# Six pairs with seven products in every block, other far pairs, and new assumptions of the planner

## The chip, the cores and the metric

The kernel runs on one core of one Trainium2 chip. The metric is the device time of one execution in microseconds (us); where several runs are shown, their median. TensorE (PE) multiplies, VectorE (DVE) and ScalarE (ACT) work on whole tiles, GpSimd (POOL) does small sums and issues some of the transfers, SyncE (SP) issues the others.

## The reference, cut to what matters

Two layers of an encoder trunk on 256 tokens of width 4096. Each layer normalises its input, multiplies it by one wide matrix, runs attention and a two-way retention on the parts of the result, and multiplies what comes out by a second matrix:

```python
for l in range(DEPTH):                       # DEPTH = 2
    h = rmsnorm(x, norm_w[l])
    proj = h @ w_in[l]                       # (256 x 4096) @ (4096 x 11264)
    aq, ak, av, ag, rq, rk, rv, rg = jnp.split(proj, SPLIT_POINTS, axis=-1)
    ...                                      # rotary embedding, 16 query and 4 key heads
    a_out = jax.nn.silu(ag) * gqa_attention(aq, ak, av)
    r = bidirectional_retention(rq, rk, rv, log_gf, log_gb)   # 8 heads
    r_out = jax.nn.silu(rg) * rmsnorm(r, ret_norm[l])
    x = x + jnp.concatenate([a_out, r_out], axis=-1) @ w_out[l]   # (256 x 4096) @ (4096 x 4096)
return rmsnorm(x, final_norm)
```

Everything is float32. The two projections are nearly all of the work, and all 4096 x 15360 weights of a layer are read once.

## The kernel before, in words

**Blocks.** A block of the program makes 256 rows by 1024 columns of a projection. Each layer has 11 blocks for `w_in` and 4 for `w_out`, 30 blocks in all. Within a block the program goes over the 4096 inner rows in 16 pairs of 256 (`NP`, numbered 0 to 15). One pair in one block is a product of two-by-two halves: 2 halves of tokens, 2 of inner rows, 2 of columns.

**Three matmuls for one product.** A float32 factor is split into a high part that TensorE multiplies exactly enough and a low part that is what remains: `whi` and `wlo` of the weights, `x8h` and `x8l` (or `x7h` and `x7l`) of the other operand. A product is high by high, low by high and high by low: two matmuls in line 1458 with `whi`, one in line 1468 with `wlo`, each with 512 columns. Products on the same page are taken up to four together (`TOGETHER`): first the matmuls with `whi` of all four, then those with `wlo`.

**Seven or eight products.** The two-by-two product of a pair takes eight products (`EIGHT_PRODUCTS`) in the plain way, or seven (`SEVEN_PRODUCTS`) with sums of the halves on either side, in the manner of Strassen. The results gather over all pairs in seven accumulators `M1` to `M7`. At the end of a block `combine` adds them up into the pages `ca` and `cb` on DVE. The pairs with seven products need sums of their weights in each block: `Weights.begin` makes `wsum` with one subtraction of 1024 columns and two operations of 512, and their weights then fill four pages (A, T, B with one half, U) in place of two (A, B). Which pairs take seven is written in two names: `SEVEN` holds for all blocks, `MORE` for the blocks of `w_out` alone. `GROUPS` cuts the row of pairs ahead of each pair with seven products, and `pages_of` lays the pages of the other pairs of a group between the four pages of its first.

**Where the parts are made.** A weight page arrives in `wraw` (transfers of SP), ACT copies it to `whi`, DVE subtracts to get `wlo` (`Weights.parts`). Five pages (`RING`) are in hand at a time; when the last product on a page is done, the page five places on is begun. For one page per far pair (`FAR_PAIRS`, page B) DVE does nothing: ACT writes `fhi`, then minus `fhi` into `flo`, and a transfer of POOL's queue adds the weights from memory onto `flo` (`far_parts`, line 505). There is one buffer for such a page (`FAR`).

**The planner.** The program is written out as one fixed order for each engine. While it is written, a clock (`now.t`) and the times until which DVE and ACT are thought busy (`ve.until`, `ac.until`) are kept with assumed costs. After each product `tick` asks `Weights.room` whether a step of other work fits: the splitting of operands, the attention and retention tasks, the postponed `thirds`. `V_FIXED` and `S_FIXED` are the fixed costs of one instruction of DVE and ACT in this reckoning, `STEP_V` and `STEP_S` the time that a step is allowed, `LANDING`, `STORE`, `FETCH` and `FAR_LANDING` the times allowed for transfers, `EARLY` how far ahead of its operands a step may be placed, `ADD_AHEAD` how far ahead of ACT an accumulating transfer may be placed, `TIGHT_A` and `TIGHT_B` the number of products at the start and the end of a block in which steps are held back. The cost of DVE is

```python
return V_FIXED + n * (0.00052 if one else 0.00104)    # one: a copy or an operation with a scalar
```

**Start and end.** In the first block two pairs (`NATIVE`) are multiplied whole, as they come, and the first two blocks (`PLAIN`) do without the split difference `x3` of the operand, which is made later, in steps of `third`. In the last block five pairs (`DELAYED`) keep the weights of their last product in places of operands that are done with; `dead_room` says which.

**Between the layers.** `out_tasks` adds the residual with an accumulating transfer to both pages of a block of `w_out`, and `out_task` then squares, stores and transposes each.

Of the kernel before, what the change touches and what calls it, by code (L numbers as in the profile page):

```python
# [32 lines left out]
NP = KT // 2  # L33
# [6 lines left out]
FAR = 1  # L40

STEP_V = 1.6
STEP_S = 1.3

V_FIXED = 0.15
S_FIXED = 0.12

MM = {512: 0.2268, 256: 0.1177}
PASS = 0.2

LANDING = 11.0
STORE = 8.0
FETCH = 13.0
FAR_LANDING = 11.0
MARGIN = 0.0

RUSH = 1.5

EARLY = 0.7

ADD_AHEAD = 2.5

NEED = {"ak": 4, "ag": 3, "rk": 4, "rg": 4}

PE_REST = 1.5

TIGHT_A = 3
TIGHT_B = 5

AT_ONCE = 2  # L70

# [3 lines left out]

START = 1

SEVEN = (0, 3, 6, 9, 12)

MORE = (1,)  # L80

DELAYED = tuple([_p for _p in range(NP) if _p not in SEVEN + MORE][-5:])

# [5 lines left out]

DEFER = (0,)  # L90

FAR_PAIRS = (2, 5, 8, 11, 14)


AQ, AK, AV, AG, RQ, RK, RVO, RG = 0, 2048, 2560, 3072, 5120, 6144, 7168, 9216
# [75 lines left out]

SEVENS = (SEVEN, tuple(sorted(SEVEN + MORE)))
EIGHTS = [_p for _p in range(NP) if _p not in SEVENS[1]]
# [19 lines left out]
def is_far(group, p, k):  # L193

    return k == PAGE_B and p in FAR_PAIRS

# [14 lines left out]
PLAIN_ORDER = ("M3", "M8", "M4", "M2")  # L211

EASY = ("M7",)

TOGETHER = 4
BANKS = ("M1", "M2", "M3", "M4", "M5", "M6", "M7", "M8")
# [35 lines left out]
def vector_cost(name, n, kwargs):  # L252
    one = name in ("tensor_copy", "tensor_scalar", "tensor_scalar_mul", "tensor_scalar_add", "memset")
    return V_FIXED + n * (0.00052 if one else 0.00104)

# [6 lines left out]
def hybrid_encoder(  # L262
# [15 lines left out]
    now = Now()  # L278
# [16 lines left out]
    def t(pool, shape, tag, bufs=None, dt=F32):  # L295
        kw = {} if bufs is None else {"bufs": bufs}
        return pool.tile(shape, dt, tag=tag, name=tag, **kw)

    def f32(v):
        return v.bitcast(F32)  # L300
# [4 lines left out]
    def own(n):  # L305

        if current[0]:
            current[0].own += n

    def drop(n=1):  # L310

        held[0] -= n
        own(-n)

    def page(shape, name, dt=F32):

        held[0] += 1
        own(1)
        assert held[0] <= PAGES, name
        return sp.tile(shape, dt, tag="pg", name=name, bufs=PAGES)  # L320
# [78 lines left out]
    class Weights:  # L399
# [92 lines left out]
        def far_parts(self, g, src):  # L492
# [6 lines left out]
            for h in halves:  # L499
                ac.activation(g.lo[h], f32(g.hi[h]), AF.Copy, scale=-1.0)  # L500
            g.high_at, g.low_at = ac.until, ac.until + FAR_LANDING

# [50 lines left out]
        def add(self, now_all=False):  # L553

            while self.adds and (now_all or self.adds[0][0] <= now.t + ADD_AHEAD):
                self.adds.pop(0)[1]()

        def room(self, using):
# [13 lines left out]
            if tight[0] and max(ve.until, ac.until) > now.t + 0.3:  # L572
                return False
            return (
                max(ve.until, now.t) + STEP_V + low <= limit
                and max(ac.until + STEP_S, free) + 1.05 + low <= end
            )

    rooms = []

    def dead_room():

        if not rooms:
            e, o = len(EIGHTS), len(SEVENS[1])
            kinds = {
                "x3": ("x3", e, [P, 2, 2, P], "p k s t -> p (k s t)"),
                "x8h": ("x8h", e, [P, 2, SEQ], "p k s -> p (k s)"),
                "x8l": ("x8l", e, [P, 2, SEQ], "p k s -> p (k s)"),
                "x7h": ("x7h", o, [P, 7, P], "p k t -> p (k t)"),
                "x7l": ("x7l", o, [P, 7, P], "p k t -> p (k t)"),  # L590
            }
            order = "x7h x7l x3 x3 x7h x7l x7h x7l x3 x8h x8l x7h x7l x3 x8h x8l x7h x7l x3 x7h" if MORE else "x3 x3 x8h x8l x3 x3 x8h x8l x7l x7h x3 x3 x8h x8l x3 x3 x8h x8l x7l x7h"
            rooms.extend(kinds[v] for v in order.split())
        tag, bufs, shape, flat = rooms.pop(0)
        return t(ap, shape, tag, bufs, F32R).rearrange(flat)[:, :NB]

# [228 lines left out]
    class Lane:  # L825
# [5 lines left out]
        def step(self):  # L831
# [17 lines left out]
            else:  # L849
                self.ready = max(self.last - EARLY, now.t + (rest or 0.1))  # L850

# [64 lines left out]
    def turned(src, room):  # L916

        ve.transpose(
            room.rearrange("p (b k t) -> p b k t", b=4, t=BLK),
            src.rearrange("p m (i b e) -> p b (m i) e", i=4, e=BLK),
        )

    def store(room, to):

        to = to.rearrange("(b e) (a f) -> a e b f", e=BLK, a=4)
        for a in range(4):  # L930
            nc.gpsimd.dma_start(to[a], room[BLK * a : BLK * (a + 1), :].rearrange("e (b f) -> e b f", b=4))
        drop()
# [65 lines left out]
    def rotary(v, L, kind, to):  # L998

        scaled(v, L)  # L1000
        yield
        C, S = L.tables.get(kind) or rope_tables(kind, L.plain)
        v4 = v.rearrange("p m (h d) -> p m h d", h=4)
        if kind in ("aq", "ak"):
            rs = t(sp, [P, 8], "rs", 3)
            for m in range(MT):
                for h in range(4):
                    ac.activation(
                        junk[:, :HD], v4[:, m, h], AF.Square, accum_out=rs[:, 4 * m + h : 4 * m + h + 1]
                    )  # L1010
                yield
            rsqrt(rs, rs, 8, HD)
        o = page([P, MT, NB], "rot")
        o4 = o.rearrange("p m (h d) -> p m h d", h=4)
        for m in range(MT):
            src = v[:, m, :].rearrange("p (h a b e) -> p h a b e", h=4, a=2, b=2)
            dsts = o[:, m, :].rearrange("p (h a b e) -> p h a b e", h=4, a=2, b=2)
            s5 = S[:, m, :].rearrange("p (a b e) -> p a b e", a=2, b=2)
            for h in range(2):
                ve.tensor_mul(  # L1020
                    dsts[:, :, :, h, :],
                    src[:, :, :, 1 - h, :],
                    s5[:, :, h, :].unsqueeze(1).to_broadcast([P, 4, 2, HD // 4]),
                )
            ve.tensor_mul(
                v4[:, m], v4[:, m], C[:, m, :].unsqueeze(1).to_broadcast([P, 4, HD])
            )
            yield
        ve.tensor_add(o, o, v)
        if kind == "ak":  # L1030
            yield
            o8 = o.rearrange("p m (h d) -> p (m h) d", d=HD)
            ve.tensor_mul(o8, o8, rs.unsqueeze(2).to_broadcast([P, 8, HD]))
        yield
        v = v.rearrange("p m n -> p (m n)")
        turned(o, v)
        drop()
        yield 0.0
        store(v, to)
        return rs if kind == "aq" else None  # L1040
# [16 lines left out]
    def attention_pair(g, h, kv, qT, rs, done):  # L1057
# [40 lines left out]
        store(room, p_dram[2 * (g % 2) + h // 2])  # L1098
        yield STORE

# [25 lines left out]
    def attention_group(L, g, gacc, qacc):  # L1126
# [11 lines left out]
        rs = yield from rotary(qacc, L, "aq", q_dram[g % 2])  # L1138
        yield STORE
        L.rs[g] = rs  # L1140
# [206 lines left out]
    def block(after_pair, phase, then, first_order=False, order=LAST_ORDER, last=None, plain=False, hurried=False):  # L1347
# [16 lines left out]
        if not first_order:  # L1364
            for b in reversed(EASY):
                n = next(i for i, v in enumerate(flat) if v[0] == b and v[1] == 0)
# [72 lines left out]
        while n < len(flat):  # L1439
# [5 lines left out]
            for one in group:  # L1445
                m, name, p, index, k, h = one
                tight[0] = m < TIGHT_A or m >= len(flat) - TIGHT_B
                a = begin_product(*one)
# [64 lines left out]
    def load_gain(n):  # L1513
        g = page([P, 2, NB], "gain")
        nc.sync.dma_start(g[:, 0, :], final_norm[columns(n)].partition_broadcast(P))
        return g
# [4 lines left out]
    def out_task(l, n, res):  # L1521

        last = l == DEPTH - 1
        if last:
            fn = load_gain(n)
            outs[n] = res
            own(-1)
            yield LANDING
            room = fn[:, 1:2, :].to_broadcast([P, MT, NB])
            fn = fn[:, 0, :]  # L1530
        else:
            turn = page([P, KG * SEQ], "room")
            room = turn.rearrange("p (m n) -> p m n", m=MT)
        for m in range(MT):
            ac.activation(room[:, m, :], res[:, m, :], AF.Square, accum_out=sums[:, m, n : n + 1])
        yield
        if last:
            ve.tensor_mul(res, res, fn.unsqueeze(1).to_broadcast([P, MT, NB]))
            drop()
            return  # L1540
        if n == N_OUT - 1:
            rstd_of(layers[l + 1], sums[:, :, :N_OUT], N_OUT)
        nc.gpsimd.dma_start(x2_dram[n].rearrange("p (m n) -> p m n", m=MT), res)
        yield
        turned(res, turn)
        if n < N_OUT - 2:
            drop()
            yield 0.0
            store(turn, next_dram[n])
            put(n, None, 2 * l + 2)  # L1550
        else:
            yield LANDING - 2.0
            to = res.rearrange("p m n -> p (m n)")
            yield from move(turn, to)
            drop()
            put(n, to, 2 * l + 2)

    def out_tasks(l, n, c):
        for i in range(2):
            nc.gpsimd.dma_start(c[i], residual(l, 2 * n + i), accum_op=ALU.add)  # L1560
        yield LANDING
        for i in range(2):
            yield from out_task(l, 2 * n + i, c[i])

    def last_combine(res):

# [147 lines left out]
    for l, L in enumerate(layers):  # L1714
        for bi, (one, _) in enumerate(BLOCKS):
# [9 lines left out]
            c = block(after, 2 * l + 1, 2 * l + 1 + (bi == N_IN - 1), start, plain=2 * l in DEFER and bi < PLAIN)  # L1725
# [7 lines left out]
        for n in range(N_OUT2):  # L1733
# [19 lines left out]
            else:  # L1753
                if final:
                    turning.append(Turn(2 * l + 2))
                c = block(after, 2 * l + 2, 2 * l + 2 + (n == N_OUT2 - 1), hurried=n == 0)
# [50 lines left out]
```

## Time and profile before

| | |
|---|---|
| time, median of 3 runs | 2625.7 us (2624.82 to 2630.23) |
| the profiled execution, its own time | 2625.96 us |
| its span, first to last instruction | 2623.8 us |
| mean granted clock of TensorE | 0.998 |
| busy: PE, DVE, ACT, POOL | 2601.0, 2166.6, 1804.2, 372.9 us |
| instructions | 34532 |
| moved by transfers | 683.94 MB, mean 261 GB/s |

The profile names a group of instructions by line, engine, operation and tiles, written out<-in. Everything that goes through the planner's clocks has line 247, so DVE and ACT work is told apart by its tiles. PE is the matmul itself, PEld the loading of its stationary operand. `x1340` is a count, and behind the bar stand the busy time in us, the mean of one in ns, and the idle time of the engine ahead of the group with what ended it. Matmuls overlap, so the duration of one (389 ns) is longer than the time from one to the next. In the views by stretch, each engine has its busy time and in brackets its instructions, then come the granted clock, the busy share of the transfer engines and what they moved.

### The profile page before, as it was taken

How to read it: one execution, taken by the hardware profiler on the slowest of the kernel's cores; microseconds unless marked ns; L12 is line 12 of the kernel's file. 1: busy time of each engine (PE TensorE's matmuls, PEld its weight loads, DVE VectorE, ACT ScalarE, POOL GpSimd, SP SyncE). 2: the span in 40 equal slices, each digit the busy share in tenths (PEclk: the TensorE clock that was granted, in tenths of full speed). 3: DMA queues.
4: the chain of work that ended last, by engine and by line, in shares of the span. 5: the costliest groups of instructions: out<-in, count | busy, mean ns of one | idle time of the engine just before them, and what ended most of it. 6: DMA issues, size and time to landing. Idle time of an engine off the chain costs nothing.

```text
span 2623.8 us, 34532 instructions
## 1 busy us (share of the span) xinstructions
PE 2601.0 (99%) x11725; PEld 2154.2 (82%) x11725; DVE 2166.6 (83%) x2684; ACT 1804.2 (69%) x2576; POOL 372.9 (14%) x510
## 2 busy tenths in 40 slices
PE   9999999999999999999999999999999999999998
PEld 7788888888888888888878888888888888888886
DVE  7898887798778898877978878888887688987876
ACT  8676676667565788655877666776576557876655
POOL 0012211221111101111111111211210111010000
PEclk9999999999999999999999999999999999999999
DMA  9988888887778777889988888888877787788887
GB/s 305 285 262 285 272 271 284 270 269 243 235 238 249 239 249 237 274 262 281 311 246 259 271 274 283 266 273 288 280 231 217 245 258 239 221 259 264 254 249 228
DMA packets 201121, 683.94 MB, mean 261 GB/s; under 512 B 24176, under 2 KB 30832, under 8 KB 200944
## 3 DMA queue, kind: packets, MB, share of 16 engines
q1 hardware_dynamic: 147760, 521.27, 56.3%
q0 software_dynamic: 53184, 160.46, 26.5%
q8 instruction: 92, 1.51, 0.2%
q14 instruction: 85, 0.70, 0.1%
HBM read 637.60 MB, written 44.04 MB: 260 GB/s over the span
## 4 chain that ended last, share of the span: by engine, by line
PE 92%; issue 1%; DMA 1%; ACT 1%; DVE 1%; POOL 0%; POOLq 0%; DVEq 0%; ACTq 0%
PE M L1458 59%; PE M L1468 30%; PE ps L973 1%; PE ps L974 1%; PE ps L975 1%; DMA q<-q_dram 1%; PE ps L1458 0%; DMA wraw<-in_w_in 0%; DVE wlo L247 0%; ACT ca L247 0%; DVE ca L247 0%; PE ps L1468 0%; DVE cb L247 0%; ACT pr L247 0%; ACT whi L247 0%
## 5 line engine op out<-in xcount | busy, mean ns | idle before, releaser
L247 ACT CAST whi<-wraw 128x1024 fp32r<-128x1024 f32 (+1 forms) x808 | 768.7, 962 | 463.0 <-PE M L1458 310.3
L247 DVE TENSOR_TENSOR wlo<-wraw,whi 128x1024 fp32r<-128x1024 f32 (+1 forms) x808 | 886.9, 1110 | 236.6 <-ACT whi L247 230.9
L1458 PE MATMUL M<-whi,x8h 128*128 128x512 f32 x1340 | 521.9, 389 | 0.0
L1458 PE MATMUL M<-whi,x8l 128*128 128x512 f32 x1340 | 521.5, 389 | 0.0
L1458 PE MATMUL M<-whi,x7h 128*128 128x512 f32 x1265 | 493.9, 390 | 3.7 <-DVE ca L247 2.5
L1458 PE MATMUL M<-whi,x7l 128*128 128x512 f32 x1265 | 492.9, 390 | 0.0
L247 ACT CAST whi<-wsum 128x1024 fp32r<-128x1024 f32 x314 | 329.6, 1050 | 137.1 <-PE M L1458 93.8
L1468 PE MATMUL M<-wlo,x8h 128*128 128x512 f32 x1340 | 420.2, 389 | 0.0
L247 DVE TENSOR_TENSOR wlo<-wsum,whi 128x1024 fp32r<-128x1024 f32 x314 | 382.5, 1218 | 38.7 <-ACT whi L247 36.8
L1468 PE MATMUL M<-wlo,x7h 128*128 128x512 f32 x1265 | 407.8, 389 | 1.1 <-DVE wlo L247 1.1
L1458 PEld LDWEIGHTS M<-whi,x8h 128*128 128x128 f32 x1340 | 251.6, 188 | 51.7 <-issue 0.2
L1458 PEld LDWEIGHTS M<-whi,x8l 128*128 128x128 f32 x1340 | 251.6, 188 | 51.7 <-issue 0.2
L1468 PEld LDWEIGHTS M<-wlo,x8h 128*128 128x128 f32 x1340 | 251.2, 188 | 51.7
L1458 PEld LDWEIGHTS M<-whi,x7h 128*128 128x128 f32 x1265 | 237.8, 188 | 55.7 <-DVE ca L247 2.9
L1468 PEld LDWEIGHTS M<-wlo,x7h 128*128 128x128 f32 x1265 | 237.5, 188 | 50.5 <-DVE wlo L247 1.5
L1458 PEld LDWEIGHTS M<-whi,x7l 128*128 128x128 f32 x1265 | 238.0, 188 | 48.9
L1458 PE MATMUL M<-whi,x 128*128 128x512 f32 x840 | 258.9, 389 | 0.7 <-ACT whi L247 0.7
L505 POOL DMA_DIRECT2D flo<-in_w_in x108 | 97.3, 901 | 1044.4 <-ACT flo L247 1001.4
L247 ACT CAST fhi<-wraw 128x1024 fp32r<-128x1024 f32 (+1 forms) x148 | 154.7, 1045 | 99.8 <-PE M L1458 93.9
L247 DVE TENSOR_TENSOR wsum<-wraw 128x1024 f32<-128x1024 f32 x157 | 191.2, 1218 | 18.7 <-DMA wraw<-in_w_out 11.3
L1458 PEld LDWEIGHTS M<-whi,x 128*128 128x128 f32 x840 | 157.1, 188 | 32.9 <-ACT whi L247 1.1
L1458 PE MATMUL M<-fhi,x8h 128*128 128x512 f32 x440 | 171.3, 389 | 0.0
(301 smaller groups left out, 3282.9 us busy)
## 6 DMA issues: line engine op xcount, KB each, us to landing
wraw<-in_w_in SPq DMA_DIRECT2D x700, 512.0 KB, 5.0
wraw<-in_w_out SPq DMA_DIRECT2D x256, 512.0 KB, 5.2
flo<-in_w_in POOLq DMA_DIRECT2D x108, 512.0 KB, 7.9
flo<-in_w_out POOLq DMA_DIRECT2D x38, 512.0 KB, 8.8
full<-next_dram POOLq DMA_DIRECT2D x18, 512.0 KB, 7.7
p_dram<-room POOLq DMA_DIRECT2D x64, 128.0 KB, 4.6
pT<-p_dram POOLq DMA_DIRECT2D x16, 512.0 KB, 8.1
next_dram<-room POOLq DMA_DIRECT2D x40, 128.0 KB, 5.9
```

Source lines behind the costliest of these rows:

```text
L247: return call(out, *args, **kwargs)
L505: nc.gpsimd.dma_start(g.lo[h], g.src[0][:, h, :], accum_op=ALU.add)
L973: nc.tensor.matmul(out, a[0], b[0], start=start, stop=False)
L974: nc.tensor.matmul(out, a[0], b[1], start=False, stop=False)
L975: nc.tensor.matmul(out, a[1], b[0], start=False, stop=stop)
L1458: nc.tensor.matmul(acc[name], a[i], g.hi[h], start=m == first[name] and not i, stop=False)
L1468: nc.tensor.matmul(acc[name], a, g.lo[h], start=False, stop=m == final[name])
```

## The change

Six pairs instead of five take seven products in the blocks of `w_in`, and the blocks of `w_out` have the same six: `SEVEN` becomes (0, 3, 6, 9, 11, 13), `MORE` is empty (before, `w_out` had 0, 1, 3, 6, 9, 12). The far pairs are 2, 5, 8, 12, 15. `dead_room` works out its list of places from the pairs, and `out_tasks` lets the first page go on without the second (with `APART` at zero, both transfers are still issued at once). Nine assumptions of the planner have other values.

```diff
-STEP_S = 1.3
+STEP_S = 1.7
-V_FIXED = 0.15
+V_FIXED = 0.08
...
-STORE = 8.0
+STORE = 6.0
...
-FAR_LANDING = 11.0
+FAR_LANDING = 10.0
...
-EARLY = 0.7
-ADD_AHEAD = 2.5
+EARLY = 0.4
+ADD_AHEAD = 0.5
...
-TIGHT_A = 3
-TIGHT_B = 5
+TIGHT_A = 4
+TIGHT_B = 4
...
-SEVEN = (0, 3, 6, 9, 12)
-MORE = (1,)
+SEVEN = (0, 3, 6, 9, 11, 13)
+MORE = ()
...
-FAR_PAIRS = (2, 5, 8, 11, 14)
+FAR_PAIRS = (2, 5, 8, 12, 15)
...
+APART = 0.0
...
-            order = "x7h x7l x3 x3 x7h x7l ..." if MORE else "x3 x3 x8h x8l ..."
-            rooms.extend(kinds[v] for v in order.split())
+            for p in range(NP):
+                if p not in EIGHTS:
+                    rooms.extend(kinds[v] for v in ("x7h", "x7l"))
+                else:
+                    rooms.extend(kinds[v] for v in ("x3", "x8h", "x8l")[: 3 if p in EIGHTS[2:] and p not in DELAYED else 1])
...
     def out_tasks(l, n, c):
         for i in range(2):
             nc.gpsimd.dma_start(c[i], residual(l, 2 * n + i), accum_op=ALU.add)
-        yield LANDING
-        for i in range(2):
-            yield from out_task(l, 2 * n + i, c[i])
+            if i < 1:
+                yield APART
+        second = now.t + LANDING
+        yield max(0.0, LANDING - APART)
+        yield from out_task(l, 2 * n, c[0])
+        yield max(0.0, second - now.t)
+        yield from out_task(l, 2 * n + 1, c[1])
```

More of the change, by code (lines that the diff above doesn't have):

```diff
@@ L591, in dead_room @@
             }
-            order = "x7h x7l x3 x3 x7h x7l x7h x7l x3 x8h x8l x7h x7l x3 x8h x8l x7h x7l x3 x7h" if MORE else "x3 x3 x8h x8l x3 x3 x8h x8l x7l x7h x3 x3 x8h x8l x3 x3 x8h x8l x7l x7h"
-            rooms.extend(kinds[v] for v in order.split())
+            for p in range(NP):
[3 more added lines that the diff above has]
+                    rooms.extend(kinds[v] for v in ("x3", "x8h", "x8l")[: 3 if p in EIGHTS[2:] and p not in DELAYED else 1])
         tag, bufs, shape, flat = rooms.pop(0)
```

## The prediction

> **What bounds the kernel now.** I read the page first (busy shares and the chain that ended last), then the list of who waited for whom on TensorE, then busy time by stretch, then the groups of instructions by form. From the page:
>
> ```profile
> span 2623.8 us, 34532 instructions
> PE 2601.0 (99%) x11725; PEld 2154.2 (82%) x11725; DVE 2166.6 (83%) x2684; ACT 1804.2 (69%) x2576; POOL 372.9 (14%) x510
> PE 92%; issue 1%; DMA 1%; ACT 1%; DVE 1%; POOL 0%; POOLq 0%; DVEq 0%; ACTq 0%
> ```
>
> TensorE (PE) is busy for all but 22.8 us of the span, and the chain that ended last is 92% TensorE. So the time is the number of matmuls times their spacing, plus few waits. VectorE (DVE) is the second engine, with 457 us free on average over the span. The waits of TensorE:
>
> ```profile
> engine line waited for: us in total, times, longest us
> PE M L1468 <- DVE wlo L247: 2.8, 2, 1.7
> PE M L1458 <- DVE ca L247: 2.5, 3, 1.0
> ...
> PE M L1458 <- DVE cb L247: 1.2, 1, 1.2
> ...
> PE M L1458 <- ACT whi L247: 0.7, 1, 0.7
> ```
>
> `wlo` and `whi` are the low and high halves of a weight page; `ca` and `cb` are the adds that empty the accumulators at the end of a block. These four come to 7.2 us in the whole execution, over 30 blocks. Where the slack of DVE is thin shows by stretch:
>
> ```profile
> core 0: us, PE busy (x) PEld busy (x) DVE busy (x) ACT busy (x) POOL busy (x), PEclk, DMA share, GB/s
> 15.00:40.00 25.00, 25.00 (x101) 18.68 (x100) 24.55 (x39) 23.37 (x42) 1.03 (x1) 1.00 0.97 360
> 40.00:80.00 40.00, 40.00 (x178) 33.14 (x177) 35.07 (x49) 34.10 (x57) 1.74 (x2) 1.00 0.92 292
> 80.00:120.00 40.00, 37.71 (x159) 30.46 (x158) 33.28 (x49) 26.66 (x46) 3.41 (x5) 0.96 0.82 269
> 120.00:160.00 40.00, 40.00 (x178) 33.14 (x177) 37.87 (x70) 27.92 (x48) 5.66 (x6) 1.00 0.88 247
> 160.00:200.00 40.00, 39.41 (x173) 32.02 (x172) 38.61 (x55) 28.77 (x48) 8.40 (x13) 1.00 0.86 264
> ...
> 960.00:1060.00 100.00, 100.00 (x456) 83.19 (x455) 91.07 (x125) 80.71 (x129) 8.98 (x9) 1.00 0.76 237
> ...
> 1345.00:1378.00 33.00, 30.54 (x134) 24.65 (x133) 22.79 (x32) 31.33 (x56) 3.03 (x4) 1.00 0.80 236
> ...
> 2493.00:2558.00 65.00, 65.00 (x288) 53.87 (x287) 48.59 (x51) 36.49 (x39) 5.22 (x6) 1.00 0.84 248
> ```
>
> In the first 200 us, where operands, weights and the postponed thirds are all made, DVE is busy 169.4 of the 185 us from 15 to 200, and there TensorE loses time (80 to 120, 160 to 200). At 960 to 1060, a change of stage, DVE is busy 91 of 100 us and TensorE loses nothing. In a plain stretch (2493 to 2558) DVE has 16 us of 65 to spare.
>
> **Term 1: fewer matmuls.** Before, five pairs take 7 products in blocks of the input projection and a sixth (pair 1) only in those of the output projection; after, six do in both. So each of the 22 input blocks loses one product, which is three matmuls of 512 columns: 22 x 3 = 66. The built programs agree: 11709 matmuls before, 11643 after, and the 66 missing are all 128x512. Their price is the spacing, not their modelled duration: in the row 2493 to 2558, 65.00 us hold 288 matmuls of this size with no gap, 0.2257 us each. 66 x 0.2257 = 14.9 us, all on the path that ends last, since TensorE is that path.
>
> The Trainium skill ("TensorE: Matmul & The Clock Gate", Part 1, on the 56 ns gap) gives 215.7 ns from start to start for a warm matmul of 512 columns; the row's 225.7 ns is higher, so this trace differs. By the page term 1 would be an estimated 14.2 us.
>
> **Term 2: more work on DVE and ScalarE (ACT).** The rows by form that price it:
>
> ```profile
> L247 DVE TENSOR_TENSOR wlo<-wraw,whi 128x1024 fp32r<-128x1024 f32 x643 | 781.9, 1219 | 226.5 <-ACT whi L247 221.3 <-PE M L1458 2.4 <-PE M L1468 0.9
> L247 ACT CAST whi<-wraw 128x1024 fp32r<-128x1024 f32 x643 | 672.5, 1050 | 408.9 <-PE M L1458 263.4 <-DMA wraw<-in_w_in 52.9 <-DMA wraw<-in_w_out 51.0
> L247 DVE TENSOR_TENSOR wlo<-wsum,whi 128x1024 fp32r<-128x1024 f32 x314 | 382.5, 1218 | 38.7 <-ACT whi L247 36.8 <-PE M L1468 1.5
> L247 ACT CAST whi<-wsum 128x1024 fp32r<-128x1024 f32 x314 | 329.6, 1050 | 137.1 <-PE M L1458 93.8 <-DVE wsum L247 37.0 <-PE M L1468 5.1
> L247 DVE TENSOR_TENSOR wsum<-wraw 128x1024 f32<-128x1024 f32 x157 | 191.2, 1218 | 18.7 <-DMA wraw<-in_w_out 11.3 <-DMA wraw<-in_w_in 7.4
> L247 DVE TENSOR_TENSOR wlo<-wraw,whi 128x512 fp32r<-128x512 f32 x165 | 113.0, 685 | 10.1 <-ACT whi L247 9.6 <-issue 0.2
> L247 DVE TENSOR_TENSOR wsum<-wsum,wraw 128x512 f32<-128x512 f32 x157 | 108.7, 692 | 5.5
> L247 DVE TENSOR_TENSOR wsum<-wraw,wsum 128x512 f32<-128x512 f32 x157 | 107.4, 684 | 0.1
> L247 ACT CAST whi<-wraw 128x512 fp32r<-128x512 f32 x165 | 102.0, 618 | 54.1 <-PE M L1458 46.9 <-DMA wraw<-in_w_out 6.7 <-ACT x L247 0.5
> ```
>
> A pair with 7 products needs three sums (1.22 + 0.69 + 0.68 us) and low halves of three and a half pages; a pair with 8 needs two. By count over the built programs DVE gets 22 of each sum, 44 more `wlo<-wsum`, 21 more half pages and 21 fewer whole `wlo<-wraw`: 22 x 2.594 + 44 x 1.218 + 21 x 0.685 - 21 x 1.219 = 99.4 us, or 4.5 us per input block. ACT gets 44 x 1.050 + 21 x 0.618 - 21 x 1.050 = 37.1 us. DVE then stands at 2266 of some 2609 us (87%), ACT at 1841 (71%). On average both still lie beside TensorE and cost nothing. The local sums say where they might not:
>
> - Steady input blocks. An input block of 122 products is 82.6 us of TensorE. Its weights cost DVE 6 x 6.93 (pairs of 7: three sums and 1.22 + 1.22 + 1.22 + 0.69) + 5 x 1.22 (near pages of the far pairs) + 10 x 1.22 = 59.9 us, which leaves 22.7 us for all else (27.8 before). All other DVE work is 2166.6 less 1684.7 (the six DVE rows above), 482 us over 30 blocks, 16 us each. It fits.
> - Neighbours 9, 10, 11, 12. Pairs 9 and 10 cost DVE 6.93 + 2.44 = 9.4 us against 15 products, 10.2 us; pairs 11 and 12 cost 8.2 against 10.2. The output blocks of before had it worse: pair 0 alone is followed by pair 1, also of 7, and pairs 0 to 2 cost 6.93 + 6.93 + 1.22 = 15.1 us of DVE against 22 products, 14.9 us, without TensorE waiting. That neighbourhood is gone, so the output blocks become easier. I take nothing for either.
> - The start. In the built program DVE has, by these durations and for other forms by 0.15 us plus 1.04 ns per element, 10 us more work in front of the adds that close the first block (one more pair of 7, two of the postponed thirds drawn forward, one more operand of 7) and 16 us more in front of those that close the second. Against this stand 5.4 us of free DVE time between 15 and 80, and 15.6 between 15 and 200. This doesn't fit without loss. The bounds are -3.9 us (the existing waits there, 2.3 us at 80 to 120, and 1.6 us of clock, both vanish) and +10.1 us (all of the first excess is waited for). I take +3: 10 us less the 5.4 free and less about 2 us, one page of lead, since five pages are kept in hand.
>
> The clock belongs to this place. In the row 80 to 120 its mean is 0.96; over 40 us that is 3.2 us at half rate, so 1.6 us lost, behind the 2.3 us of waits in the same row. The row 1345 to 1378 has 2.5 us of waits and a clock of 1.00, so such waits don't always do it, and I add nothing. The Trainium skill ("TensorE: Matmul & The Clock Gate", Part 1, what is happening) says that the clock halves after an idle window of about 3.4 us; this trace shows a halving behind shorter waits, so it doesn't fully agree. By the page, longer waits at the start would make halvings likelier.
>
> **Term 3: what is moved.** The far pairs become 12 and 15 in place of 11 and 14, still five per block, so the transfers stay the same in number. The relevant rows, and the last line of the answer on tile `flo`:
>
> ```profile
> 301.91 0.39 PE L1468 MATMUL M<-flo,x8h 128*128 128x512 f32 x1
> 302.52 1.06 ACT L247 ACTIVATE flo<-fhi 128x1024 fp32r<-128x1024 f32 x1
> 303.88 0.88 POOL L505 DMA_DIRECT2D flo<-in_w_in  x1 [12.55 <-ACT flo L247]
> 316.87 0.62 PE L1468 MATMUL M<-flo,x8h 128*128 128x512 f32 x2
> DMA to landing us min/median/max: 5.2/8.0/10.4
> ```
>
> There is one buffer for a far page. It comes free at 302.3, is refilled by ACT and an accumulating transfer issued at 303.88, and is needed at 316.87. The slowest landing (10.4) ends at 314.3. From 12 to 15 there are the same 19 products, but the last pair takes its products one by one, so the low half is needed six matmuls (1.35 us) earlier: 315.5. It still lands 1.2 us early, hidden by those 19 products; if ACT is late there, the cost is that lateness. ADD_AHEAD of 0.5 moves the issue behind at most 2 us of planned work on POOL's queue, which the median landing covers (311.9). Splitting out_tasks in two lets the first page go on as before and the second wait for its own landing: no matmul stands behind it. Steps for the last block's kept pages and pair 1's operands are exchanged like for like: nothing.
>
> The other constants change only where the planner places steps. V_FIXED of 0.08 makes it believe a 1024-wide subtraction takes 0.08 + 1024 x 0.00104 = 1.145 us, where the row says 1.219. So it packs DVE tighter than it runs, 0.07 us per instruction. Bounds: below, the 7.2 us of waits go; above, rival two. I take 0, because in the built program the DVE work between the first and the last accumulator add of a block falls from 239 to 212 us in sum over the 30 blocks: the page sums that stood between them moved away.
>
> **Sum.** The profiled execution took 2625.96 us, 2.2 more than its span, and 0.3 more than the median of 2625.7. 2625.96 - 14.9 + 3.0 = 2614.1; less 0.3, the median should be 2613.8. A measurement of this kernel can tell about 0.2% (5.2 us) from no change.
>
> **Rivals.** One: DVE is late at the start and also where stages change, and eats most of the gain. For it: the sums of the start, and 1345 to 1378, where 2.5 us were lost already. Its price is 10.1 us at the start, at most 16 with the second block's excess: 2621 to 2627. Against it: 960 to 1060, where 91% on DVE cost nothing. Two, on the other side: the planner's short price of DVE makes the accumulators come free late at every block. For it: `ca` and `cb` waits exist (3.7 us over 30 blocks, 0.12 each), and 93 DVE instructions a block times 0.07 us are 6.5 us unplanned. One add of 0.68 us late at each of 30 boundaries is 20.4 us: 2613.8 - 3 + 20.4 = 2631. It decides from 0.67 us per block on, where term 1 and the 5.2 us are used up. Against it: DVE idles 457 us, mostly behind `whi`, and catches up in those gaps, and fewer sums lie between the adds. That the change doesn't remove the products is ruled out by the built program.
>
> **How the numbers follow.** Forecast (start between -4 and +7): 0.80. Rival one: 0.12, two thirds of it within 0.2%. Rival two: 0.08. The range runs from 2607 (term 1 whole, and half of the 7.2 us of waits and of the clock's loss gone, -4) to 2621 (the first excess wholly waited for). Faster by over 0.2%: 0.80 and a third of rival one, less some for both in part, 0.83; within 0.2%: 0.09; slower: 0.08.
>
> **What would show it.** Right: 66 fewer matmuls, DVE busy near 2266 and ACT near 1841 us, TensorE idle 23 to 29 us with the new idle time before 200 us, `flo` waits near zero, DVE waits at block ends below 0.3 us each. Wrong: `ca`, `cb` or `wlo` waits of over 0.6 us in most blocks, clock below 1.00 after 130 us, or a `flo` wait once per block at pair 15 or pair 2.

## The result and the profile after

The changed kernel is slower: 2641.1 us (median of 4 runs) against 2625.3, a ratio of 1.0056 with a 95% interval of 1.0035 to 1.0077. That is 14.7 us slower by the ratio, where 11.9 us faster was forecast. One of the four runs (2814.4 us, at a mean clock of 0.87) was in a slower state of the chip and is left out of the ratio; the median of the other three is 2640.2 us. The profiled execution took 2642.1 us. From its page:

```profile
span 2640.3 us, 34679 instructions
...
PE 2595.8 (98%) x11659; PEld 2143.2 (81%) x11659; DVE 2250.8 (85%) x2796; ACT 1844.8 (70%) x2622; POOL 365.8 (14%) x511
...
PE 87%; DVE 3%; DMA 1%; issue 1%; ACT 1%; POOL 0%; DVEq 0%; POOLq 0%; ACTq 0%; SPq 0%
```

The 66 matmuls are gone (11725 to 11659), and DVE and ACT have about the work that was forecast (2266 and 1841 us): the six DVE rows of the weights rose by 97.2 us where 99.4 was forecast, and all other DVE work fell by 13. But TensorE is idle for 44.5 us in place of 22.8, and DVE now stands in the chain that ended last with 3%. Who made TensorE wait (line, releaser, us in total, times, longest; the lines 1463, 1473 and 249 are 1458, 1468 and 247 of the kernel before):

```profile
PE M L1463 <- DVE ca L249: 10.6, 9, 2.6
PE M L1463 <- ACT x L249: 5.2, 1, 5.2
PE M L1463 <- DVE cb L249: 4.2, 5, 1.8
PE M L1463 <- DVE x L249: 4.0, 3, 2.2
PE M L1473 <- DVE wlo L249: 2.0, 4, 1.2
PE M L1463 <- ACT flo L249: 1.7, 1, 1.7
PE M L1473 <- DMA flo<-in_w_in: 1.2, 1, 1.2
```

The waits on `ca`, `cb` and `wlo` rose from 6.5 to 16.8 us, and 9.2 us on `x` are new: `x` stands here for `x3`, the split difference of an operand, which is made at a change of stage. Busy time by stretch, where the kernel before had its thin places:

```profile
core 0: us, PE busy (x) PEld busy (x) DVE busy (x) ACT busy (x) POOL busy (x), PEclk, DMA share, GB/s
80.00:120.00 40.00, 35.32 (x147) 28.13 (x146) 34.72 (x53) 28.58 (x52) 4.90 (x7) 0.96 0.85 281
...
160.00:200.00 40.00, 38.05 (x160) 30.67 (x160) 38.15 (x50) 26.37 (x30) 6.20 (x9) 0.96 0.92 275
...
960.00:1060.00 100.00, 95.54 (x425) 77.82 (x424) 91.16 (x129) 79.46 (x128) 6.54 (x8) 0.98 0.71 219
...
1386.00:1452.00 66.00, 60.59 (x256) 49.27 (x255) 54.14 (x72) 44.71 (x69) 8.39 (x9) 0.95 0.77 234
2244.00:2310.00 66.00, 62.08 (x275) 49.91 (x274) 62.73 (x95) 54.82 (x89) 4.06 (x5) 1.00 0.71 230
```

Nearly all of the loss is at the start and at the changes of stage. That is plainest when the same point of both programs is compared: the time of the last matmul into M2 in each of the 30 blocks, after less before, worked out from the two traces (minus is earlier).

```text
blocks 0-2    input, layer 0, start         +0.5 +2.5 +4.7
blocks 3-10   input, layer 0                +2.7 +1.7 -1.6 -2.3 -2.3 -2.9 -3.6 -3.4
blocks 11-14  output, layer 0               +3.3 +4.1 +3.9 +5.9
blocks 15-25  input, layer 1               +13.3 +12.6 +11.9 +11.5 +10.8 +10.4 +9.8 +9.9 +9.2 +8.5 +8.3
blocks 26-29  output, layer 1              +14.5 +14.5 +14.5 +15.8
```

In the steady input blocks the change gains: 8.1 us over blocks 3 to 10 (3.3 of them in block 5) and 5.0 us over blocks 16 to 25, 0.5 each where 0.68 was forecast. It loses 6.7 us in block 11, 7.4 in block 15 and 6.2 in block 26, the first block of each new stage, 2.0 in block 14, and 4.7 by the end of block 2.

### The profile page after: what moved, and what is told of

The parts are those of the page before. It is cut to its first block, busy times and chain, and to the rows that moved or that the text cites. A ratio compares the mean times of both kernels' runs of the same rounds, so it can differ in the third digit from the quotient of the medians.

```text
span 2640.3 us, 34679 instructions
## 1 busy us (share of the span) xinstructions
PE 2595.8 (98%) x11659; PEld 2143.2 (81%) x11659; DVE 2250.8 (85%) x2796; ACT 1844.8 (70%) x2622; POOL 365.8 (14%) x511
## 4 chain that ended last, share of the span: by engine, by line
PE 87%; DVE 3%; DMA 1%; issue 1%; ACT 1%; POOL 0%; DVEq 0%; POOLq 0%; ACTq 0%; SPq 0%
PE M L1463 56%; PE M L1473 28%; DVE wlo L249 1%; PE ps L979 1%; PE ps L980 1%; PE ps L978 1%; DMA wraw<-in_w_out 1%; DMA x7l<-in_w_out 0%; DVE wsum L249 0%; DVE cb L249 0%; ACT whi L249 0%; DVE ca L249 0%; DVE x8l L249 0%; DVE x L249 0%; DMA wraw<-in_w_in 0%
## 5 line engine op out<-in xcount | busy, mean ns | idle before, releaser
L249 DVE TENSOR_TENSOR wlo<-wraw,whi 128x1024 fp32r<-128x1024 f32 (+1 forms) x808 | 875.3, 1095 | 168.8 <-ACT whi L249 156.1
L249 DVE TENSOR_TENSOR wlo<-wsum,whi 128x1024 fp32r<-128x1024 f32 x358 | 436.0, 1218 | 118.3 <-ACT whi L249 113.6
L249 ACT CAST whi<-wsum 128x1024 fp32r<-128x1024 f32 x358 | 375.6, 1049 | 143.3 <-PE M L1463 95.6
L1473 PE MATMUL M<-wlo,x8h 128*128 128x512 f32 x1336 | 414.7, 390 | 1.2 <-DVE wlo L249 1.2
L1473 PE MATMUL M<-wlo,x7h 128*128 128x512 f32 x1253 | 414.7, 390 | 0.9 <-DVE wlo L249 0.8
L249 DVE TENSOR_TENSOR wsum<-wraw 128x1024 f32<-128x1024 f32 x179 | 217.6, 1216 | 7.2 <-DMA wraw<-in_w_out 6.2
```

Source lines behind the costliest of these rows:

```text
L249: return call(out, *args, **kwargs)
L1473: nc.tensor.matmul(acc[name], a, g.lo[h], start=False, stop=m == final[name])
```

## The experiments

All runs are compared with runs of the kernel before on the same chip. "The changed kernel" is 1.0056 in these ratios.

**Pairs or assumptions.** Two runs take the two halves of the change apart: the eight assumptions with other values (`APART`, at zero, moves nothing in time), and the pairs with all the rest, which is the far pairs, `dead_room` and `out_tasks`. No run parts these last from the pairs.

```diff
 changed kernel, pairs as changed:
-STEP_S = 1.7, V_FIXED = 0.08, STORE = 6.0, FAR_LANDING = 10.0, EARLY = 0.4, ADD_AHEAD = 0.5, TIGHT_A = 4, TIGHT_B = 4
+STEP_S = 1.3, V_FIXED = 0.15, STORE = 8.0, FAR_LANDING = 11.0, EARLY = 0.7, ADD_AHEAD = 2.5, TIGHT_A = 3, TIGHT_B = 5
```

> The changed kernel with the eight assumptions of the planner as they were before (STEP_S, V_FIXED, STORE, FAR_LANDING, EARLY, ADD_AHEAD, TIGHT_A, TIGHT_B); the pairs and far pairs as changed. Theory A (the planner's new assumptions pack DVE too tightly where it has no slack, and the 30 us lost at the start and at the changes of stage come from that): most of the loss goes, 2611 to 2618 us. Theory B (the pairs themselves bring the loss, since the seventh product's sums fill DVE at the start and at the changes of stage, whatever the planner assumes): 2633 to 2643 us, with the first block after each change of stage still 6 us late.

Measured: 2677.5 us, ratio 1.0199 (1.0185 to 1.0213). The reverse, old pairs with new assumptions:

> The kernel before with the eight new assumptions of the planner and its own pairs. Theory A: the loss shows without the pairs, 2640 to 2655 us. Theory B: about the time of before, 2622 to 2630 us.

Measured: 2646.3 us, 1.0080 (1.0068 to 1.0093). The first lies in neither range, the second in that of theory A, so neither theory fits both. The assumptions alone cost 0.8%, the pairs alone 2.0%, both together 0.56%. The new assumptions are a cure for the new pairs, not the illness: with the new pairs they save 36 us.

**The price of DVE in the planner.** One value at a time, with the changed pairs, and once with the old ones:

```diff
-V_FIXED = 0.08
+V_FIXED = 0.15      # then 0.0; then 0.08 with the other seven as before; then 0.08 in the kernel before
```

> The changed kernel with V_FIXED alone set back to 0.15, so that the planner's price of a DVE instruction of 1024 columns is 1.215 us, as the profile has it. Theory A in its narrow form (the short price of DVE does it): 2612 to 2622 us. Theory B, or theory A through another of the assumptions: 2636 to 2643 us, as the changed kernel.

> The changed kernel with V_FIXED of 0.0 in place of 0.08 (0.15 gave 2681.8). Theory P: the forced operand steps go on falling, 2625 to 2637 us. Theory D: with still more packed in, the waits for ca, cb and wlo outgrow that, 2642 to 2665 us.

> The changed pairs, all assumptions as before except V_FIXED, which has its new 0.08 (all old: 2677.5; all new: 2641.1). If V_FIXED alone carries the gain of the new assumptions: 2636 to 2648 us. If the others are needed with it: 2655 to 2677 us.

> The kernel before with V_FIXED of 0.08 alone (all new assumptions: 2646.3). Theory D: the optimistic price makes DVE late and carries most of that loss, 2636 to 2650 us. Theory P: with the old pairs there is room anyway, so the price matters little, 2620 to 2632 us, and the loss of 20.8 us is from another assumption.

Measured: 0.15 gives 2681.8 us (1.0215, 1.0201 to 1.0229), 0.0 gives 2682.6 (1.0215, 1.0198 to 1.0233), 0.08 with the other assumptions as before 2661.8 (1.0135, 1.0118 to 1.0153), and 0.08 in the kernel before 2633.8 (1.0030, 1.0020 to 1.0041). So with the new pairs both a dearer and a cheaper price lose 41 us more, which no theory had in its range, and they lose it in different places. The 0.08 alone brings 16 of the 36 us; the other seven are needed with it. With the old pairs its 8 us lie between the two ranges and leave most of the 20.8 us to the other seven. Waits of TensorE at 0.15:

```profile
PE M L1463 <- ACT x L249: 31.0, 5, 10.1
PE M L1463 <- DVE ca L249: 14.3, 14, 3.8
PE M L1463 <- DVE cb L249: 3.7, 6, 1.5
PE M L1473 <- DVE wlo L249: 3.5, 2, 2.5
```

and at 0.0:

```profile
PE M L1473 <- DVE wlo L249: 18.3, 16, 4.6
PE M L1463 <- DVE ca L249: 12.0, 10, 2.5
PE M L1463 <- ACT x L249: 5.7, 1, 5.7
```

The program's text offers a reading: at the true price the planner sees no room and postpones operand steps, and the first product that needs the operand forces them while TensorE stands (`x`, 31 us in five waits, all in blocks 11, 15 and 26); at a price of nothing it packs so much in that the weights' low halves come late (`wlo`, 18 us in 16 waits). 0.08 stands between the two. The waits are measured, the planner's reasons are not. If both have one cause, it would be that the new pairs leave DVE too little room where operands are made; the next runs test that.

**Is it DVE's real time?** In the next run the order of the program stays and DVE gets faster: the three weight sums become copies, while the planner books the old price. The sums are left out, so it is a measurement and not the reference's computation.

```diff
+    def light(to, src):
+        ve.until = max(ve.until, now.t) + vector_cost("tensor_sub", math.prod(to.shape[1:]), {})
+        nc.vector.tensor_scalar_mul(to, src, 1.0)
...
-                ve.tensor_sub(self.v, self.a, self.b[:, 0:1, :].to_broadcast([P, 2, NB]))
+                light(self.v, self.a)
...
-                ve.tensor_add(self.u[:, 0, :], self.a[:, 1, :], self.v[:, 0, :])
-                ve.tensor_sub(self.u[:, 1, :], self.u[:, 0, :], self.b[:, 1, :])
+                light(self.u[:, 0, :], self.v[:, 0, :])
+                light(self.u[:, 1, :], self.u[:, 0, :])
```

> The changed kernel in its own order, with the three weight sums of each pair of seven replaced on DVE by copies of one operand (times 1.0), for which the planner still books the full price; the sums are left out, so this is not the result of the reference. The order of all other instructions stays, DVE gets lighter by perhaps 0.5 us for each 1024 columns, 150 to 250 us in all. Theory D (at the start and at the changes of stage the real DVE runs late, and TensorE waits for it at ca, cb and wlo): most of these 16.8 us go and with them the halved clock, 2612 to 2625 us. Theory P (the planner, finding no room on DVE, postpones operand steps until the next stage forces them, so the loss sits in the order): the waits for x (9.2 us) and the time stay, 2632 to 2642 us.

Measured: 2618.5 us, 0.9972 (0.9960 to 0.9984), which is 22 us less than the changed kernel by the ratios. From its page, from the groups by form (first the changed kernel's row), and the waits of TensorE:

```profile
PE 2587.2 (99%) x11659; PEld 2141.8 (82%) x11659; DVE 2084.5 (80%) x2796; ACT 1845.1 (70%) x2622; POOL 370.2 (14%) x511
```

```profile
L249 DVE TENSOR_TENSOR wsum<-wraw 128x1024 f32<-128x1024 f32 x179 | 217.6, 1216 | 7.2 <-DMA wraw<-in_w_out 6.2 <-DVE pTl L249 0.7 <-DMA wraw<-in_w_in 0.3
...
L401 DVE TENSOR_SCALAR wsum<-wraw 128x1024 f32<-128x1024 f32 x179 | 123.0, 687 | 0.0
```

```profile
PE M L1468 <- DVE ca L249: 5.3, 7, 1.1
PE M L1468 <- ACT x L249: 5.2, 1, 5.2
PE M L1478 <- DMA flo<-in_w_out: 2.5, 2, 1.3
PE M L1468 <- DVE x L249: 2.3, 3, 1.0
...
PE M L1478 <- DVE wlo L249: 0.5, 1, 0.5
PE M L1468 <- DVE cb L249: 0.3, 2, 0.2
```

DVE has 166 us less, the waits on `ca`, `cb` and `wlo` fall from 16.8 to 6.1 us, and the end of block 2, which came 4.7 us later than in the kernel before, comes 5.0 us earlier. The time lies in theory D's range. Two things keep this from being a proof. The copies don't read the second weight page, so the 6.5 us are gone too for which DVE waited for transfers there. And light sums may help any order. Two runs go with it, the kernel before with the same light sums, and the light sums booked at a light price:

> The kernel before, in its own order, with the same lighter sums on DVE (the true sums are left out). It lost 7 us to waits for ca, cb, wlo and whi. Theory D (only with the new pairs does DVE run late): 2615 to 2624 us, a gain of at most 10 us against the 22.7 us that the changed kernel gained by it. If lighter sums speed up any order alike: 2600 to 2608 us.

> The lighter sums of the earlier run (copies of one operand; the true sums are left out), and now the planner books them at the lighter price too (0.08 us plus 0.52 ns per element), so that it may place more. The run with the full price booked gave 2618.5, with 5.2 us left waiting for x at one change of stage and 15 us lost over the changes of stage. Theory P (what is left there is operand steps postponed for want of room in the planner's book): the wait for x goes and the time is 2605 to 2614 us. Theory D alone (DVE's true time decides, the book hardly): 2615 to 2625 us.

Measured: the kernel before with light sums 2611.6 us (0.9934, 0.9920 to 0.9947), between the two ranges; booked light 2642.2 (1.0047, 1.0034 to 1.0059). The first says that the kernel before also loses to late DVE, 17 us by the ratio and 14 between the profiled executions, more than the 10 that I allowed (DVE's 18.7 us of waits for the second page are gone in it too). Of its waits on `ca`, `cb`, `wlo` and `whi` one is left:

```profile
PE M L1463 <- DVE ca L247: 0.4, 1, 0.4
```

So of the 22 us that light sums gave the changed kernel only 5 to 7 are its own, and with light sums in both the changed pairs are still the slower ones by 0.4%. The blocks show where, by the same reckoning as above, both kernels with light sums, changed less before:

```text
blocks 0-2    input, layer 0, start         -0.2 +0.2 -0.4
blocks 3-10   input, layer 0                -1.5 -2.5 -3.6 -4.2 -4.7 -5.4 -6.1 -6.8
blocks 11-14  output, layer 0               -2.1 -2.1 -2.1 +1.4
blocks 15-25  input, layer 1               +10.2 +9.6 +8.9 +8.2 +7.5 +6.8 +6.2 +5.7 +5.0 +4.3 +3.7
blocks 26-29  output, layer 1               +8.0 +8.0 +8.0 +8.0
```

At the start the 4.7 us are gone, and in blocks 0 to 2 of the changed kernel DVE has no wait of this kind for a second page: theory D is shown for that part. The steady blocks 16 to 25 gain 6.5 us, 0.65 each, nearly the forecast three matmuls. But blocks 11, 14, 15 and 26 still lose 4.7, 3.5, 8.8 and 4.3 us, 21.3 in all, where with true sums they lost 22.3. There the faster sums closed hardly any of the gap. The changed kernel with light sums keeps 65 us more DVE work than its twin (2084.5 against 2019.7 us), so a part of the 21.3 can still be DVE, and the order of the steps is the other candidate; no run separates them for blocks 11 and 26. The second run refutes theory P as I put it: told that there is more room, the planner fills it (waits on `cb` of 11.9 us), and the wait of 5.2 us on `x` stays.

**The wait of 5.2 us on x.** In the changed kernel this wait ends at 1397.55. The timeline of ACT ahead of it (start, duration, engine, instruction, and in brackets the idle time before it):

```profile
1392.38 1.71 ACT L249 ACTIVATE cb<-cb,nw 128x256 f32<-128x256 f32 x4
1393.98 0.57 ACT L249 COPY ca<-M 128x512 f32<-128x512 f32 x1
1394.45 1.05 ACT L249 CAST whi<-wraw 128x1024 fp32r<-128x1024 f32 x1
1395.39 1.32 ACT L249 CAST x8h<-cb 128x256 fp32r<-128x256 f32 x4
1397.09 0.41 ACT L249 CAST x<-cb 128x256 fp32r<-128x256 f32 x1 [0.37 <-DVE cb L249]
```

DVE's row of the same time, and from the answer on tile `cb` from 1330 to 1393 the copies that fill the page (durations, then first and last start):

```profile
1395.84 0.76 DVE L249 TENSOR_TENSOR x8l<-cb,x8h 128x256 fp32r<-128x256 f32 x2 [2.02 <-ACT x8h L249]
...
L249 ACT COPY cb<-room x16: 383/403/407, 1372.8 to 1385.6; 32x256 f32<-32x256 f32 x16
```

All steps of an operand (gains, high part, then DVE's difference for which ACT waits 0.37 us, and the high part of that) stand behind each other, and TensorE waits for the last. DVE isn't late here: it stands idle for 2.02 us in the midst of the wait. Nor is the page: its last copy ends at 1386.0, 6.4 us before the gains begin (1.5 us in the kernel before), and ACT fills these 6.4 us with weight pages. So the steps stand late in ACT's order. I took it for the layout of the last group, which needs pair 14 four products earlier than before, and moved its pages:

```diff
+    late = 2 if group[-1] == NP - 1 else 0
     for _i, _v in enumerate(one):
-        order += [_v] + rest[_i : _i + 1]
-    return order + rest[len(one) :]
+        order += [_v] + (rest[_i - late : _i - late + 1] if _i >= late else [])
+    return order + rest[max(0, len(one) - late) :]
```

> The changed kernel with the pages of the last group (pairs 13, 14, 15) in another order: those of 14 and 15 come two places later between those of 13, so that pair 14 is needed five products (3.4 us) later in each block. Theory L (the wait of 5.2 us for x at the change of layer is a chain of fixed length from the last output block to pair 14's operand, and the new layout needs it too early): that wait falls to about 2 us and the halved clock behind it goes, 2632 to 2638 us. If the wait comes from DVE or from the planner's book: it stays at 5 us, 2639 us or more.

Measured: 2675.1 us, 1.0184 (1.0162 to 1.0205), and the wait on `x` is 5.4 us. The trace shows that the edit puts three products in front of pair 14, not five, so 2.0 us and not 3.4; by theory L the wait should still have shrunk by that. It didn't, so theory L falls. The wait has the length of the row of steps, and it showed in most runs with the new last group at 5.2 to 5.7 us, whatever the load, the price or the order. That the steps stand together at that place, with their data long there, is seen; why the planner gave them no earlier place is not settled.

**Other pairs, other far pairs.** The same number of products with pair 1 in place of 11 and 13, and the last far pair moved:

```diff
-SEVEN = (0, 3, 6, 9, 11, 13)
-FAR_PAIRS = (2, 5, 8, 12, 15)
+SEVEN = (0, 1, 3, 6, 9, 12)         # first run, with FAR_PAIRS = (2, 5, 8, 11, 14)
+FAR_PAIRS = (2, 5, 8, 12, 14)       # second run, with SEVEN as changed
```

> The same number of products as the changed kernel with its new assumptions, but pairs 0, 1, 3, 6, 9, 12 in all blocks and the far pairs of before, so that the last group (12 to 15) is as before. Theory L: no wait for x at the change of layer, but pairs 0 to 2 cost DVE 15.1 us against 14.9 of TensorE at the head of every block; 2630 to 2645 us. Theory D alone: the head of the block, right behind the accumulator adds, is the worst place for two pairs of seven, 2650 us or more.

> The changed kernel with 14 as the last far pair in place of 15. Theories A and B: within 3 us of the changed kernel's 2641. Theory C (with pair 15 far, the transfer onto the low part lands late or ACT's two passes for it fall into the end of the block, where the accumulators are emptied): the loss at the ends of blocks goes, 2625 us or less.

Measured: 2731.4 us (1.0407, 1.0389 to 1.0425) and 2790.1 us (1.0621, 1.0606 to 1.0635). The first lies in theory D's range, but doesn't show its cause: the largest sum of waits is 32.1 us, for far pages in transfer (`flo<-in_w_in`), against 19.3 on `ca`, `cb` and `wlo`, and it did not free the changes of stage: 16.9 us of waits on `x`. The second tests something other than I meant. Between the uses of `flo` of 12 and 14 lie only 11 products and the eight matmuls on `fhi`, 41 matmuls or 9.3 us, while the one buffer takes 9.4 us to fill again even with a median landing (from 302.5 to 311.9 in the trace of before). Its waits:

```profile
PE M L1473 <- DVE wlo L249: 75.2, 33, 4.6
PE M L1473 <- DMA flo<-in_w_in: 31.2, 15, 5.2
PE M L1473 <- DMA flo<-in_w_out: 8.1, 3, 4.2
```

The 39 us on `flo` are the price of a far page that comes too soon. The 75 us on `wlo` come once in nearly every block, at its head, also in blocks without a wait on `flo`; with 15 no longer far, DVE has one low half more to make at the end of a block, but that this is their cause was not tested. So it is no clean test of pair 15. The mean granted clock of that run is 0.974.

**Relief at the start.** Two of the four small sums of each operand on GpSimd, and a third plain block so that the postponed thirds have more time:

```diff
-            ve.tensor_sub(s1, a22n, x1[:, 0])
+            nc.gpsimd.tensor_tensor(s1, a22n, x1[:, 0], op=ALU.subtract)
...
-            ve.tensor_sub(s3, x0[:, 0], x1[:, 0])
+            nc.gpsimd.tensor_tensor(s3, x0[:, 0], x1[:, 0], op=ALU.subtract)
```

```diff
-PLAIN = 2
+PLAIN = 3           # in the kernel before, and in the changed kernel
```

> The changed kernel with two of the four small sums of each operand of seven (s1 and s3, 128 columns, at the start and at the changes of stage) made by GpSimd in place of DVE; the result is unchanged. Theory D: 0.57 us less on DVE for each of six operands at each of four stages, 3.4 us at each place where it is late, so 2632 to 2640 us. If GpSimd's sums come later than DVE's, or its queue then holds back the accumulating transfers: 2642 us or more.

> The kernel before with three plain blocks at the start in place of two (PLAIN = 3), so that the eleven postponed thirds have one more block. Theory D at the start (the blocks 0 to 5 lose 8 us of DVE's lateness, as the lighter sums showed): 2618 to 2624 us. If the third block's tasks lose by it (its eighth accumulator is the bank that attention and retention use): 2628 us or more.

> The changed kernel with PLAIN = 3. Theory D at the start: 4 to 8 us less than the changed kernel, 2633 to 2637 us. If the tasks of the third block lose by it: 2642 us or more.

Measured: 2645.4 us (1.0060, 1.0048 to 1.0073), 2625.1 (0.9998, 0.9989 to 1.0007) and 2654.3 (1.0109, 1.0094 to 1.0124). None helps. On GpSimd the two sums take 0.75 and 0.90 us in the mean, where a sum of that size on DVE takes 0.28; the waits on `ca` fall to 7.7 us, and those on `wlo` and `flo<-in_w_in` rise to 7.1 and 3.7. A third plain block leaves the kernel before where it was: 4.1 us are gained up to block 3 and given back by block 7. In the changed kernel it costs 13 us. No version that computes the reference's result beat the kernel before.

## Why the prediction was wrong

**Term 1, fewer matmuls: right, and the gain is there.** 66 matmuls are gone, and with light sums in both kernels ten steady blocks gain 6.5 us, 0.65 each, where 3 x 0.2257 = 0.68 was forecast.

**Term 2, the steady blocks: right in the main.** DVE and ACT rose to 2250.8 and 1844.8 us, and blocks 3 to 10 gain 8.1 us. Blocks 16 to 25 gain 5.0 us in place of 6.8, and with light sums nearly all of it, so DVE was not quite without cost there.

**Term 2, the start: too small.** +3 was taken. Up to block 2 the kernel lost 4.7 us where three blocks should have gained 2.0, so it cost 6.7, inside the stated bounds. With light sums in both kernels 1.6 of it is left, so here it was late DVE.

**Term 2, the changes of stage: this step failed.** I took nothing there, by the row 960 to 1060 of before, where DVE at 91% cost TensorE nothing. After, DVE is busy the same 91.16 us in that stretch and TensorE loses 4.5. The busy share of a stretch did not say whether the work in it came in time. It wasn't for lack of time before it either: from 930 to 945 DVE stood idle for 3.3 of the 15 us, in the kernel before for 0.7 (columns as above, first the changed kernel):

```profile
930.00:945.00 15.00, 15.00 (x68) 12.40 (x67) 11.66 (x17) 14.83 (x29) 1.43 (x2) 1.00 0.83 302
...
930.00:945.00 15.00, 15.00 (x68) 12.43 (x67) 14.34 (x22) 14.81 (x29) 0.54 (x1) 1.00 0.79 254
```

By the blocks, changes of stage cost 6.7 + 2.0 + 8.1 + 6.2 + 1.3 us (blocks 11, 14, 15 with its forecast gain added, 26, 29), 24.3 in all. With light sums in both kernels blocks 11, 14, 15 and 26 still lose 21.3 us, where they lost 22.3. The largest piece, block 15, is the wait of 5.2 us on `x` and 3.4 us of halved clock behind it, and there the operand steps stood late in ACT's order while DVE was idle. For blocks 11 and 26 the cause stays open between late DVE and late placing. Rival one had the places, and its mechanism holds for the start; its ceiling of 16 us came from the start alone.

**The clock: wrong.** I added nothing for it, though longer waits were expected at the start. The granted clock stood at half for 3.4 us from 99, 188 and 980 us on and for 6.8 from 1397, where before it did so once, from 98. By the four rows above with a clock below 1.00 (40 x 0.04 twice, 100 x 0.02, 66 x 0.05) that is 8.5 us lost against 1.6 before, so some 7 us more. It is most of why busy TensorE fell by 5.2 us and not by 14.9.

**Term 3: nearly right.** `flo` made TensorE wait 1.2 us once for the transfer and 1.7 once for ACT.

**The planner's price: taken at nothing, wrongly reasoned.** Rival two expected the short price to make the adds late at all 30 boundaries. Waits on `ca` and `cb` were 14 in number, not one per block, and the true price was worse by 41 us (16 with the other seven assumptions as before). With the old pairs the short price alone costs 0.3%.

## What to carry to other kernels

A second engine with 17% of its time free on average may have none where the stages change; before work is given to it to save work of the first, it has to be known whether its results come in time at those places, and a busy share doesn't tell it. A run in the same order, with that engine's added work made cheaper and the plan left as it was, does, if the kernel before gets the same run: alone it gave 22 us here, of which only 5 to 7 belonged to the change. Assumptions of a planner are not prices to be made true: the same short price helped one set of pairs by 41 us (16 beside the old values of the others) and harmed the other by 8, so a change of work and its plan have to be judged together.

## What the hardware showed that was not expected

The clock of TensorE is granted in steps of 3.41 us. In these traces each stretch at half clock lasts one step or a multiple of it (6.83 and 10.24 us occur), within a trace they begin a whole number of steps apart, and such a stretch comes right behind a step in which TensorE stood idle for more than about half. From the trace of the changed kernel, cut into these steps:

```profile
core 0: us, PE busy (x) PEld busy (x) DVE busy (x) ACT busy (x) POOL busy (x), PEclk, DMA share, GB/s
96.04:99.45 3.41, 1.16 (x4) 0.71 (x5) 3.38 (x7) 1.20 (x2) 0.85 (x1) 1.00 0.84 277
99.45:102.86 3.41, 3.41 (x9) 2.63 (x9) 3.41 (x5) 2.28 (x5) 0.00 (x0) 0.50 1.02 252
102.86:106.28 3.42, 3.42 (x16) 2.83 (x16) 3.02 (x6) 2.34 (x3) 0.00 (x0) 1.00 1.01 332
...
1393.10:1396.51 3.41, 0.00 (x0) 0.00 (x0) 1.39 (x4) 3.41 (x9) 0.00 (x0) 1.00 0.70 220
1396.51:1399.93 3.42, 2.15 (x4) 1.45 (x5) 3.35 (x8) 1.02 (x3) 0.00 (x0) 0.50 1.04 285
1399.93:1403.34 3.41, 3.41 (x9) 2.64 (x8) 0.06 (x1) 1.04 (x1) 0.00 (x0) 0.50 0.83 308
1403.34:1406.75 3.41, 3.41 (x16) 2.80 (x15) 3.08 (x3) 1.05 (x1) 0.00 (x0) 1.00 0.00 1
```

Behind 2.25 us of idle time in one step, the next holds 9 matmuls where the one after it holds 16. Cut in the same way, the 17 traces of this case have 101 steps at full clock with 1.95 us or more of idle time, and every one is followed by a step at half clock; of the 12871 with less than 1.5 us none is; of the 51 between, 25 are. So it is the idle time within one step that counts, not the wait as a whole. The three waits at 1320 to 1327, 3.2 us together, lie in three steps with at most 1.3 us each and brought nothing; the 3.6 us at 2285 to 2293 left 1.9 us in one step, where it can go either way, and brought nothing. Waits of some 2 us that fall into one step thus cost 1.7 us more, half of the next step.
